# A decoder step's mixing phase: the inverse as a task of its own, the delta rule later behind q's tile, block turns in two parts

## The chip, the cores and the metric

The kernel runs on one core of a Trainium2 chip. The metric is device time in microseconds for one execution of the whole program; three runs of the kernel before gave 2160.1, 2160.87 and 2161.47 us. One more execution was recorded by the hardware profiler. PE is TensorE (matrix multiply), DVE VectorE, ACT ScalarE, POOL GpSimd, SP the engine that issues most DMAs.

## The reference

One step of a hybrid decoder layer, in f32: 512 new positions of one prompt and 8 single tokens of sampled sequences (520 columns), model width 2048. The mixing half is a gated delta rule with 8 heads of 128 beside a pooling group; the second half is a SwiGLU of width 5632.

```python
def decoder_layer(h, ...):
    xn = rmsnorm(h, norm_mix)
    proj = xn @ w_in                      # q | k | v | z | beta, decay | pool
    qkv_c, new_conv = short_conv(conv_buf, proj[..., :3 * DN_WIDTH], conv_w)   # 4 taps, silu
    ...
    a_mat = m + jnp.eye(CHUNK)            # m: strict lower part of (k beta) k^T * decay
    u = triangular_solve(a_mat, v * beta)
    w = triangular_solve(a_mat, k * beta * exp(g))
    # over the chunks, with the state S carried along:
    v_new = u_i - w_i @ S
    o = q_i * exp(g_i) @ S + qk_i @ v_new
    S = S * exp(g_last) + k_dec^T @ v_new
    ...
    dn_out = rmsnorm(o, dn_norm) * silu(z)
    h = h + concat([dn_out, pool_out]) @ w_out
    ...
```

## The kernel before

**Phases.** From 0 to about 605 us the kernel projects the 520 columns: 40 tiles of 128 output columns, each 96 matmuls (`product`; lines 168 to 170: a hi/lo split of both operands in three passes, over 16 blocks of the inner dimension and two column chunks of 264 and 256). The tiles' order is k0 to k3, z0 to z3, v0, q0, v1, q1, v2, q2, v3, q3, then the same for heads 4 to 7, then the eight pool tiles p6, p7, p4, p5, p2, p3, p0, p1. From about 607 us the output product follows (lines 1178 to 1180), and from about 618 to the end the SwiGLU part, which the change does not touch.

**Weave.** The delta rule and the other small work are generators on tracks of a `Weave` object (line 45). During every tile `weave.step()` is called 16 times, after the 15th matmul, then after each sixth to the 87th, then after the 90th, 93rd and 96th. A task that yields n is gone on with n steps later. A track is worked off in order, and a task starts no sooner than its delay after it was added. So these numbers decide where PE's small matmuls stand among the projection's. PE executes in this written order. The order on the other engines is set by the framework's scheduler when the program is built, with the evictions of a tile's results (line 259) and the weight splits (lines 135 and 137) at high priority. Every engine executes its list in order.

**One head.** A k tile is convolved (DVE lines 737 and 739: four taps; ACT line 740: silu) and, in `turn_blocks` (757), turned block by block: a transpose on DVE, a store to `tok_d` and four loads back, on POOL's queue. `keys` (790) forms the strict lower matrix in `mixb` and stores its four 32x32 diagonal blocks per chunk to `nd_d`. `eliminate` (822) handles four heads at once: it loads the blocks as `nb` and inverts them by 31 steps of two DVE instructions (lines 835 and 837); then `ud_d` is written twice, plain and transposed (838 and 841). `qv_tiles` (1112) loads the inverse as `utf` for a head (line 1117), projects v and q, and adds `delta(h)`, one step later, that is from the next tile's 15th matmul. `delta` (845) first completes the 128x128 inverse: one product (859), three triangular steps (869, each followed by DVE's 871 into `uu`), beside them the product of keys and q (878); then for four chunks it runs the state recurrence: S times keys (894), R on DVE (896), W (901), the output and the next state (906, 912, 913). `states`, `sample_norms`, `sample_product` and `sample_out` (988) handle the sampled tokens and stand in the first track behind the deltas; `sample_out` writes its columns of all eight heads in `mixa` (line 1013). After it DVE forms differences of mixa's halves (L203) and splits the rows for the output product (ACT 194 `xh`, DVE 195 `xl`).

```python
            qT = d1tile("s0", [P, SEQ], "qT")
            qkv_tile(0, h, qT)
            qk = d1tile("tq", [P, SEQ], "qk")
            turn_blocks(0, h, qT, qk)
            weave.add(delta(h, qT, qk, vs), 0, 1)
```

Of the kernel before, what the change touches and what calls it, by code (L numbers as in the profile page):

```python
# [17 lines left out]
P = 128  # L18
# [24 lines left out]
class Weave:  # L43
# [3 lines left out]
    def __init__(self):  # L47
        self.tracks, self.wait, self.now = ([], []), [0, 0], 0

# [20 lines left out]
def decoder_kernel(ctx, tc, x_prompt, x_sample, state_delta, state_conv, state_pool, norm_mix, w_in,  # L70
# [186 lines left out]
    def normed_out(out, acc, c0, c1, base):  # L257

        dve.tensor_tensor(out, acc[:, c0 - base:c1 - base], rb[:out.shape[0], c0:c1], op=ALU.mult)  # L259

    def columns():
        ext = pre.tile([P, 3 + SEQ], F32, tag="ext", name="ext", bufs=2)
        pool.memset(ext[:, 0:3], 0.0)
        return ext

# [255 lines left out]
    with ExitStack() as p1:  # L521
# [234 lines left out]

        def turn_blocks(kind, h, src, dst):

            bt, d = d1tile("bt", [P, SEQ], "bt"), tok_d[kind, h]
            if kind % 2:  # L760
                dve.transpose(bt, src)
                d = d.rearrange("p f -> (p f)").rearrange("(c p f) -> c p f", c=NCH, p=P)
                pool.dma_start(d.rearrange("c p f -> p c f"), v3(bt))
                rows = d.rearrange("c (i p) (j q) -> j p (c i) q", p=32, q=32)
            else:
                dve.transpose(bt.rearrange("p (j c q) -> p c j q", j=4, c=NCH),
                              src.rearrange("p (c j q) -> p c j q", j=4, c=NCH))
                pool.dma_start(d, bt)
                rows = d.rearrange("(i p) (j f) -> j p i f", p=32, j=4)
            for j in range(4):  # L770
                pool.dma_start(dst[32 * j:32 * j + 32, :].rearrange("p (n q) -> p n q", n=rows.shape[2]), rows[j])

        def decay(h):
# [16 lines left out]
        def keys(h):  # L790
# [23 lines left out]
            for q in range(4):  # L814
                r = slice(32 * q, 32 * q + 32)
                sp.dma_start(nd_d[h, q].rearrange("c s j -> s c j"), nn3[r, :, r])
            for q in range(4):
                r = slice(32 * q, 32 * q + 32)
                pool.memset(nn3[r, :, r], 0.0)


        def eliminate(b):
            hs = slice(4 * b, 4 * b + 4)
            nb = d1tile("nb", [64, 32, 32], "nb")
            sp.dma_start(nb.rearrange("p s j -> p (s j)"), nd_d[hs].rearrange("h q c s j -> (h q c) (s j)"))
            u = d1tile("u", [64, 32, 32], "u")
            uf = u.rearrange("p s j -> p (s j)")
            yield 10
            pool.memset(uf, 0.0)
            pool.memset(uf[:, 0:1024:33], 1.0)  # L830
            for t in range(31, 0, -1):
                w = 32 - t
                tm = d1tile("tm", [64, 256], "tm")
                tv = tm[:, 0:t * w].rearrange("p (s j) -> p s j", j=w)
                dve.tensor_tensor(tv, nb[:, 0:t, t:t + 1].broadcast_to([64, t, w]),
                                  u[:, t:t + 1, t:32].broadcast_to([64, t, w]), op=ALU.mult)
                dve.tensor_tensor(u[:, 0:t, t:32], u[:, 0:t, t:32], tv, op=ALU.subtract)
# [3 lines left out]
            sp.dma_start(ud_d[hs, :, 1].rearrange("h q c s j -> (h q) c (s j)"), ut.rearrange("p s j -> p (s j)"))  # L841
            yield 1


        def delta(h, qT, qk, vs):
            kT, nn, kd = mixb[:, h % 4, 0:SEQ], mixb[:, 4 + h % 4, 0:SEQ], kds[h]
            fk, ik = sck[:, h, 0, :], sck[:, h, 1, :]
            utf = utfs[h % 2]
            udf, tdf = utf[:, 0], utf[:, 1]
            gcb, dm = decay(h)  # L850
            act.activation(gcb, gcb, AF.Exp)
            qts = d1tile("qts", [P, SEQ], "qts")
            dve.tensor_tensor(qts, qT, gcb, op=ALU.mult)

            xp = pst()
# [5 lines left out]
            pool.tensor_copy(v3(cur), udf)  # L863
            yield 2
            for it in range(3):
                yp = v3(pst())
                j = slice(32 * it + 32, P)
                for c in range(NCH):
# [3 lines left out]
                                         op0=ALU.mult, op1=ALU.add)  # L872
                if it == 0:
                    dve.tensor_tensor(v3(kd), v3(kd), bc3(sck[:, h, 2, :]), op=ALU.mult)
                if it == 2:
                    gq_ = pst()
                    for c in range(NCH):
                        te.matmul(gq_[:, ck(c)], kT[:, ck(c)], qT[:, ck(c)], start=True, stop=True)
                    aq = d1tile("aq", [P, SEQ], "aq")
                    for c in range(NCH):  # L880
                        dve.scalar_tensor_tensor(aq[:, ck(c)], gq_[:, ck(c)], fk[:, c:c + 1], dm[:, ck(c)],
                                                 op0=ALU.mult, op1=ALU.mult)
                if it == 1:
                    scaled(vs, ik)
                yield 2

            op_ = pst()
            S = None
            for c in range(NCH):
                if S is None:  # L890
                    R = by_chunk(vs)[:, c]
                else:
# [5 lines left out]
                    R = Rt  # L898
                    yield 2
                wp = pst()  # L900
# [13 lines left out]
                S = S2  # L914
                yield 1
                if c == 1:
                    ss = d1tile("ss", [P, NCH], "ss")
                    junk = d1tile("junk", [P, P], "junk")
                    for j in range(NCH):
                        act.activation(by_column(junk), by_chunk(qk)[:, j], AF.Square, accum_out=ss[:, j:j + 1])  # L920
                    dve.tensor_scalar(ss, ss, EPS, None, op0=ALU.add)
# [191 lines left out]
        def qv_tiles(h):  # L1113
            utf = utfs[h % 2].rearrange("p a c j -> p (a c) j")
            for q in range(4):
                r = slice(32 * q, 32 * q + 32)
                sp.dma_start(utf[r, :, r], ud_d[h, q].rearrange("a c s j -> s (a c) j"))
# [9 lines left out]
        kds = {}  # L1127
# [978 lines left out]
```

## Time and profile before

| what | value |
|---|---|
| median of three runs | 2160.87 us |
| the profiled execution | 2161.12 us, of it span 2159.4 |
| PE busy, share of the span | 2127.0 us, 98% |
| DVE | 1772.2 us, 82% |
| ACT | 919.9 us, 43% |
| POOL | 531.4 us, 25% |
| mean granted PE clock of the execution | 0.998 |
| PE busy from 196 to 320 us | 120.82 of 124 us |
| PE busy from 480 to 595 us | 114.68 of 115 us |
| PE busy from 660 us to the end | 1489.49 of 1499 us |

A line of a time line has the start in us, the duration, engine, source line, operation and "output<-inputs"; in brackets stands the idle time of the engine before it and what ended it. A line of a table by windows has the window, its length, the busy time of PE, PE's weight loads, DVE, ACT and POOL with their instructions, PE's granted clock, the busy share of the DMA engines and GB/s. A line of the waits has who waited for what, in all, how often, and the longest. SPq is the DMA-issuing queue of SP.

### The profile page before, as it was taken

To read this page: it belongs to the slowest core of one execution; us is meant where nothing else is said; L and a number is where in the kernel's file an instruction comes from. 1 tells how busy PE (TensorE), PEld (TensorE's weight loads), DVE (VectorE), ACT (ScalarE), POOL (GpSimd) and SP (SyncE) were. 2 spreads that over 40 slices of the span, in tenths; PEclk is the share of its full clock that TensorE was granted. 3 is DMA by queue.
4 is the path that set the end of the run, shared out by engine and by line. 5 is a ranking of instruction groups with operands and counts; after the bars stand their busy time and mean duration, and the time that the engine had idled before them with its cause. 6 is when DMAs were issued, how large, how long until landed. Compare 5 with 4: busy or idle time off the path is not lost.

```text
span 2159.4 us, 43083 instructions
## 1 busy us (share of the span) xinstructions
PE 2127.0 (98%) x17681; PEld 2118.4 (98%) x17681; DVE 1772.2 (82%) x2715; ACT 919.9 (43%) x1340; POOL 531.4 (25%) x672
## 2 busy tenths in 40 slices
PE   8999999999999999999999999999999999999998
PEld 7999999999999999999999999999999999999998
DVE  7886677667599979988988988988877898887997
ACT  6433433343264544434434434434334444435444
POOL 2413441332012202233233233232113302003100
PEclk9999999999999999999999999999999999999999
DMA  8444454544445533554554454454456746438333
GB/s 281 126 125 118 130 141 122 132 125 126 122 118 162 156 114 115 150 167 141 144 164 144 143 168 142 142 169 133 121 147 189 233 112 205 115 104 248 91 108 119
DMA packets 449154, 313.84 MB, mean 145 GB/s; under 512 B 29116, under 2 KB 425813, under 8 KB 445613
## 3 DMA queue, kind: packets, MB, share of 16 engines
q1 hardware_dynamic: 422733, 219.94, 36.5%
q0 software_dynamic: 24912, 90.34, 13.4%
q8 instruction: 139, 2.28, 0.5%
q10 hardware_dynamic: 1312, 0.80, 0.1%
q14 instruction: 58, 0.48, 0.1%
HBM read 259.86 MB, written 51.82 MB: 144 GB/s over the span
## 4 chain that ended last, share of the span: by engine, by line
PE 82%; DVE 9%; DMA 3%; issue 2%; ACT 2%; POOL 1%; SPq 0%; DVEq 0%; ACTq 0%; POOLq 0%
PE dn L1252 21%; PE dn L1251 21%; PE dn L1253 21%; PE mm L168 5%; PE mm L169 5%; PE mm L170 5%; DVE lo L1245 1%; DMA vs<-tok_d 1%; DVE lo L137 1%; DVE y L739 1%; DMA st<-a_d 1%; DVE raw L1273 1%; PE dn L869 1%; DMA tok_d<-bt 1%; ACT hi L1244 0%
## 5 line engine op out<-in xcount | busy, mean ns | idle before, releaser
L1245 DVE TENSOR_TENSOR lo<-raw,hi 128x1024 fp32r<-128x1024 f32 (+1 forms) x422 | 527.9, 1271 | 89.0 <-ACT hi L1244 86.8
L1244 ACT CAST hi<-raw 128x1024 fp32r<-128x1024 f32 (+1 forms) x422 | 427.8, 1027 | 401.2 <-DVE raw L1273 195.5
L168 PE MATMUL mm<-xh,hi 128*128 128x256 f32 (+1 forms) x1280 | 380.3, 297 | 1.8 <-DVE mixa L259 1.8
L169 PE MATMUL mm<-xl,hi 128*128 128x256 f32 (+1 forms) x1280 | 362.1, 283 | 0.9 <-DVE xl L350 0.5
L170 PE MATMUL mm<-xh,lo 128*128 128x256 f32 (+1 forms) x1280 | 362.2, 283 | 0.4 <-DVE lo L137 0.4
L168 PEld LDWEIGHTS mm<-xh,hi 128*128 128x128 f32 x1280 | 242.1, 189 | 3.0 <-DVE mixa L259 2.2
L169 PEld LDWEIGHTS mm<-xl,hi 128*128 128x128 f32 x1280 | 242.3, 189 | 1.7 <-DVE xl L350 1.7
L170 PEld LDWEIGHTS mm<-xh,lo 128*128 128x128 f32 x1280 | 241.3, 189 | 0.6 <-DVE lo L137 0.6
L1252 PE MATMUL dn<-b21l,hi 128*128 128x260 f32 x620 | 175.8, 284 | 0.3 <-DVE b21l L1815 0.3
L1253 PE MATMUL dn<-b21h,lo 128*128 128x260 f32 x620 | 175.4, 283 | 0.0
L1251 PE MATMUL dn<-b21h,hi 128*128 128x260 f32 x620 | 175.0, 282 | 0.0
L1253 PE MATMUL dn<-b11h,lo 128*128 128x260 f32 x612 | 173.2, 283 | 1.3 <-DVE lo L1245 1.3
L1273 DVE TENSOR_TENSOR raw<-raw 128x1024 f32<-128x1024 f32 (+1 forms) x130 | 172.0, 1323 | 2.2
L1437 POOL TENSOR_TENSOR mixa<-mixa 128x520 f32<-128x520 f32 x22 | 50.2, 2280 | 501.6 <-DVE mixa L1431 501.6
L1252 PE MATMUL dn<-b11l,hi 128*128 128x260 f32 x612 | 173.3, 283 | 0.0
L1251 PE MATMUL dn<-b11h,hi 128*128 128x260 f32 x612 | 172.7, 282 | 0.0
L1251 PE MATMUL dn<-T1h,hi 128*128 128x260 f32 x556 | 158.1, 284 | 0.0
L1252 PE MATMUL dn<-T1l,hi 128*128 128x260 f32 x556 | 157.7, 284 | 0.0
L1253 PE MATMUL dn<-T1h,lo 128*128 128x260 f32 x556 | 156.7, 282 | 0.0
L1251 PE MATMUL dn<-B22h,hi 128*128 128x260 f32 x548 | 155.9, 284 | 0.0
L1252 PE MATMUL dn<-B22l,hi 128*128 128x260 f32 x548 | 155.6, 284 | 0.0
L1253 PE MATMUL dn<-B22h,lo 128*128 128x260 f32 x548 | 154.6, 282 | 0.4 <-DVE lo L1245 0.4
(664 smaller groups left out, 6552.6 us busy)
## 6 DMA issues: line engine op xcount, KB each, us to landing
raw<-in_w_gate_up_dram SPq DMA_DIRECT2D x134, 512.0 KB
raw<-in_w_in_dram SPq DMA_DIRECT2D x79, 512.0 KB
a_d<-mixa POOLq DMA_DIRECT2D x22, 1040.0 KB, 5.5
raw<-in_w_down_dram SPq DMA_DIRECT2D x48, 448.0 KB
mixb<-in_w_gate_up_dram SPq DMA_DIRECT2D x41, 512.0 KB
raw<-in_w_out_dram SPq DMA_DIRECT2D x25, 512.0 KB
st<-a_d POOLq DMA_DIRECT2D x49, 260.0 KB, 6.4
raw<-in_w_down_dram SPq DMA_DIRECT2D x24, 512.0 KB
```

The lines of the kernel that those rows point to most:

```text
L137: dve.tensor_tensor(lo[:, r], raw[:, r], hi[:, r].bitcast(F32), op=ALU.subtract)
L168: te.matmul(acc[ci], wh, hi[k][:, c0:c1], start=(k == 0), stop=False)
L169: te.matmul(acc[ci], wh, lo[k][:, c0:c1], start=False, stop=False)
L170: te.matmul(acc[ci], wl, hi[k][:, c0:c1], start=False, stop=(k == len(w) - 1))
L739: dve.scalar_tensor_tensor(y, ext[:, i:i + SEQ], cw(i, t), y, op0=ALU.mult, op1=ALU.add)
L1244: act.copy(hi, raw)
L1245: dve.tensor_tensor(lo, raw, hi.bitcast(F32), op=ALU.subtract)
L1251: te.matmul(acc, wh[:, k, :], xf[:, k, :], start=start and k == 0, stop=False)
L1252: te.matmul(acc, wh[:, k, :], xg[:, k, :], start=False, stop=False)
L1253: te.matmul(acc, wl[:, k, :], xf[:, k, :], start=False, stop=stop and k == wh.shape[1] - 1)
L1273: dve.tensor_tensor(r[name], r[a], r[b], op=op)
L1437: pool.tensor_tensor(q[:, 4:8:2, :], q[:, 1:4:2, :], q[:, 0:2, :], op=ALU.subtract)
```

## The change

- `delta` is cut in two. `solve(h)` completes the inverse in a track of its own; it is added before v's tile with a delay of 8 steps, or 24 for the first head of a block. Its steps stand 3, 4, 4 and 1 weave steps apart, and at its end the keys are scaled and the decay rows loaded. `delta(h)` begins with the product of keys and q, 6 steps behind q's tile (8 for the first head of a block), and its chunks have one more step of space.
- `turn_blocks` becomes the generator `turn` on a track of its own: transpose and store, then 6 steps, then the four loads. It starts 5 steps after v's and k's tiles, 9 after q's, 7 after the delta rule.
- `eliminate` yields 15 and not 10, and a copy of one column that z's second tile of the block writes (`mix[4 * b + 1]`) into the array holds it until then. The clearing of the diagonal blocks becomes a task too (`cleared`).
- The three zero columns ahead of the convolution are set once in two fixed buffers and not for each tile; the squares of q come a chunk later; the pool product of the last group waits 30 steps and not 12.

```diff
-        self.tracks, self.wait, self.now = ([], []), [0, 0], 0
+        self.tracks, self.wait, self.now = ([], [], [], [], []), [0] * 5, 0
...
+    exts = [pre.tile([P, 3 + SEQ], F32, tag="ext", name="ext", bufs=2) for _ in range(2)]
+    for ext in exts:
+        pool.memset(ext[:, 0:3], 0.0)
+
     def columns():
-        ext = pre.tile([P, 3 + SEQ], F32, tag="ext", name="ext", bufs=2)
-        pool.memset(ext[:, 0:3], 0.0)
-        return ext
+        exts.append(exts.pop(0))
+        return exts[1]
...
-        def turn_blocks(kind, h, src, dst):
+        def turn(kind, h, src, dst):
...
+            yield 6
+            if kind == 0:
+                dst = qks[h] = d1tile("tq", [P, SEQ], "qk")
             for j in range(4):
                 pool.dma_start(dst[32 * j:32 * j + 32, :].rearrange("p (n q) -> p n q", n=rows.shape[2]), rows[j])
+            if kind == 3:
+                weave.add(gate(h, dst), 3, 8)
+
+        def query_rows(h, qT):
+            yield from turn(0, h, qT, None)
+
+        def key_rows(h):
+            kds[h] = d1tile("kd", [P, SEQ], "kd")
+            yield from turn(1, h, mixb[:, h % 4, 0:SEQ], kds[h])
...
+            weave.add(cleared(h), 2, 5)
...
-            yield 10
+            yield 15
+            pool.tensor_copy(uf[:, 0:1], mix[4 * b + 1][:64, NB:NB + 1])
             pool.memset(uf, 0.0)
...
-        def delta(h, qT, qk, vs):
-            kT, nn, kd = mixb[:, h % 4, 0:SEQ], mixb[:, 4 + h % 4, 0:SEQ], kds[h]
-            fk, ik = sck[:, h, 0, :], sck[:, h, 1, :]
+        def solve(h):
+            kT, nn = mixb[:, h % 4, 0:SEQ], mixb[:, 4 + h % 4, 0:SEQ]
...
-            yield 2
+            yield 3
             for it in range(3):
...
-                if it == 2:
-                    gq_ = pst()
...
-                if it == 1:
-                    scaled(vs, ik)
-                yield 2
+                yield 4 if it < 2 else 1
+            kd = kds[h]
+            dve.tensor_tensor(v3(kd), v3(kd), bc3(sck[:, h, 2, :]), op=ALU.mult)
+            gcb, dm = decay(h)
+            act.activation(gcb, gcb, AF.Exp)
+            solved[h] = cur, gcb, dm
+
+        def delta(h, qT, vs):
+            kT, nn, kd = mixb[:, h % 4, 0:SEQ], mixb[:, 4 + h % 4, 0:SEQ], kds[h]
+            fk, ik = sck[:, h, 0, :], sck[:, h, 1, :]
+            cur, gcb, dm = solved[h]
+            gq_ = pst()
+            for c in range(NCH):
+                te.matmul(gq_[:, ck(c)], kT[:, ck(c)], qT[:, ck(c)], start=True, stop=True)
...
+            dve.tensor_tensor(qts, qT, gcb, op=ALU.mult)
+            scaled(vs, ik)
+            yield 4
...
-                    yield 2
+                    yield 3
...
-                yield 1
-                if c == 1:
+                yield 2
+                if c == 2:
...
-            turn_blocks(3, h, on, on)
-            weave.add(gate(h, on), 1, 12)
+            weave.add(turn(3, h, on, on), 2, 7)
...
+            weave.add(solve(h), 4, 8 if h % 4 else 24)
             vs = d1tile("vs", [P, SEQ], "vs")
             qkv_tile(2, h, vs)
-            turn_blocks(2, h, vs, vs)
+            weave.add(turn(2, h, vs, vs), 2, 5)
             qT = d1tile("s0", [P, SEQ], "qT")
             qkv_tile(0, h, qT)
-            qk = d1tile("tq", [P, SEQ], "qk")
-            turn_blocks(0, h, qT, qk)
-            weave.add(delta(h, qT, qk, vs), 0, 1)
+            weave.add(query_rows(h, qT), 2, 9)
+            weave.add(delta(h, qT, vs), 0, 6 if h % 4 else 8)
...
-                kds[h] = d1tile("kd", [P, SEQ], "kd")
-                turn_blocks(1, h, mixb[:, h % 4, 0:SEQ], kds[h])
+                weave.add(key_rows(h), 2, 5)
...
-                weave.add(pool_mix(t // 2, *splits[t // 2]), 1, 12 if t > 1 else 7)
+                weave.add(pool_mix(t // 2, *splits[t // 2]), 1, 30 if t == 7 else 12 if t > 1 else 7)
```

The lines move: what was 825 (nb's load), 835 and 837 (elimination), 859, 869, 878, 894, 901 and 906 is now 845, 856 and 858, 872, 882, 899, 916, 923 and 928; 739, 740, 754 and 766 are now 742, 743, 757 and 769; 1008 and 1013 are 1029 and 1034; 1117 is 1138. PE has as many matmuls as before. Head 0's first product of the inverse (859, now 872) stood behind the 15th matmul of v1's tile and stands behind the 57th of q0's; for the heads of a block after the first, the product of keys and q (878, now 899) stood behind the 51st matmul of the tile after q's and stands behind the 45th; the sample's sum (1008, now 1029) stood behind the 63rd of p0 and stands behind the 15th of p1.

The order on SP's queue around the first inverse, before, from the last keys' blocks to the loads of `utf` (645 and 647 are its two buffers; `raw` is a weight load):

```order
L816 DMA nd_d<-mixb 32x4x32 x3
L131 DMA raw<-in_w_in_dram 128x8x128
L816 DMA nd_d<-mixb 32x4x32
L776 DMA gcb<-gcr_d 128x512
L825 DMA nb<-nd_d 64x1024
L131 DMA raw<-in_w_in_dram 128x8x128 x6
L838 DMA ud_d<-u 16x4x1024
L841 DMA ud_d<-ut 16x4x1024
L131 DMA raw<-in_w_in_dram 128x8x128
L1117 DMA utf_645<-ud_d 32x8x32 x3
L131 DMA raw<-in_w_in_dram 128x8x128
L1117 DMA utf_645<-ud_d 32x8x32
```

The same place of the queue now:

```order
L838 DMA nd_d<-mixb 32x4x32 x4
L798 DMA gcb<-gcr_d 128x512
L131 DMA raw<-in_w_in_dram 128x8x128
L845 DMA nb<-nd_d 64x1024
L131 DMA raw<-in_w_in_dram 128x8x128 x6
L859 DMA ud_d<-u 16x4x1024
L862 DMA ud_d<-ut 16x4x1024
L131 DMA raw<-in_w_in_dram 128x8x128
L1138 DMA utf_645<-ud_d 32x8x32 x4
```

The four stores of the last keys' blocks follow each other, and so do the four loads of head 0's inverse; the weight load that stood among each of them has moved.

DVE's order at the end of q2's tile, before (`vs` is v, `ext` and `y` are q2's columns and taps):

```order
L934 TENSOR_TENSOR ro<-ro,fq 128x4
L936 TENSOR_TENSOR mixb<-dn,ro 128x512
L259 TENSOR_TENSOR ext<-mm,rb 128x256
L761 STREAM_TRANSPOSE bt<-mixb 128x512
L137 TENSOR_TENSOR lo<-raw,hi 128x1024
L737 TENSOR_SCALAR y<-ext,prm 128x512
L754 TENSOR_TENSOR vs<-vs,sck 128x512
L739 SCALAR_TENSOR_TENSOR y<-ext,prm,y 128x512 x3
```

The same place now:

```order
L259 TENSOR_TENSOR ext<-mm,rb 128x256
L740 TENSOR_SCALAR y<-ext,prm 128x512
L757 TENSOR_TENSOR vs<-vs,sck 128x512
L137 TENSOR_TENSOR lo<-raw,hi 128x1024
L742 SCALAR_TENSOR_TENSOR y<-ext,prm,y 128x512
L933 SCALAR_TENSOR_TENSOR S<-S,egl,dn 128x128
L742 SCALAR_TENSOR_TENSOR y<-ext,prm,y 128x512
L953 TENSOR_TENSOR so<-so,ro 128x4
L742 SCALAR_TENSOR_TENSOR y<-ext,prm,y 128x512
L954 TENSOR_SCALAR so<-so 128x4
L956 TENSOR_TENSOR ro<-ro,fq 128x4
L958 TENSOR_TENSOR mixb<-dn,ro 128x512
```

The output's scaling and turn (936 and 761, now 958 and 764) have moved behind q's taps; the scaling of v has moved ahead of the weight split.

DVE's order at the end of the mixing phase, before, from the sample's last columns of `mixa` on:

```order
L1013 SCALAR_TENSOR_TENSOR mixa<-sc_u,prm,mixa 128x8x8
L203 TENSOR_TENSOR mixa<-mixa 128x4x260 x2
L259 TENSOR_TENSOR pe_7283<-mm,rb 128x256
L1072 TENSOR_TENSOR pes<-pe_7283 128x512
L137 TENSOR_TENSOR lo<-raw,hi 128x1024
L1075 TENSOR_TENSOR pes<-pes,rcnt 128x1
L137 TENSOR_TENSOR lo<-raw,hi 128x1024
L1077 SCALAR_TENSOR_TENSOR pw<-pes,pe_7283 128x512
L195 TENSOR_TENSOR xl<-mixa,xh 128x520 x2
```

The same now, with the sample's small steps ahead of it:

```order
L1039 COPY sc_u<-dn 64x128
L195 TENSOR_TENSOR dl<-pw,dh 128x520
L220 RECIPROCAL sc_u<-sc_u 128x64
L221 TENSOR_TENSOR sc_u<-sc_u 128x64
L222 TENSOR_TENSOR sc_u<-sc_u 128x64
L223 TENSOR_SCALAR sc_u<-sc_u 128x64
L224 TENSOR_TENSOR sc_u<-sc_u 128x64
L1033 TENSOR_TENSOR sc_u<-sc_u 128x64
L1034 SCALAR_TENSOR_TENSOR mixa<-sc_u,prm,mixa 128x8x8
L203 TENSOR_TENSOR mixa<-mixa 128x4x260 x2
L137 TENSOR_TENSOR lo<-raw,hi 128x1024
L195 TENSOR_TENSOR xl<-mixa,xh 128x520
```

p0's second eviction, its pool taps and two weight splits stood behind the sample's columns and stand ahead of them; before the splits of mixa's rows (195) only one weight split is left, and p1's evictions fall among them.

More of the change, by code (lines that the diff above doesn't have):

```diff
@@ L769, in turn_blocks, with cleared @@
                 rows = d.rearrange("(i p) (j f) -> j p i f", p=32, j=4)
+            yield 6
+            if kind == 0:
+                dst = qks[h] = d1tile("tq", [P, SEQ], "qk")
             for j in range(4):
                 pool.dma_start(dst[32 * j:32 * j + 32, :].rearrange("p (n q) -> p n q", n=rows.shape[2]), rows[j])
+            if kind == 3:
[5 more added lines that the diff above has]
+            yield from turn(1, h, mixb[:, h % 4, 0:SEQ], kds[h])
+        def cleared(h):
+            nn3 = v3(mixb[:, 4 + h % 4, 0:SEQ])
+            for q in range(4):
+                r = slice(32 * q, 32 * q + 32)
+                pool.memset(nn3[r, :, r], 0.0)
+            yield 1
         def decay(h):
@@ L816, in keys @@
                 sp.dma_start(nd_d[h, q].rearrange("c s j -> s c j"), nn3[r, :, r])
-            for q in range(4):
-                r = slice(32 * q, 32 * q + 32)
-                pool.memset(nn3[r, :, r], 0.0)
+            weave.add(cleared(h), 2, 5)
         def eliminate(b):
@@ L842, in eliminate @@
             yield 1
-        def delta(h, qT, qk, vs):
-            kT, nn, kd = mixb[:, h % 4, 0:SEQ], mixb[:, 4 + h % 4, 0:SEQ], kds[h]
-            fk, ik = sck[:, h, 0, :], sck[:, h, 1, :]
+        def solve(h):
+            kT, nn = mixb[:, h % 4, 0:SEQ], mixb[:, 4 + h % 4, 0:SEQ]
             utf = utfs[h % 2]
             udf, tdf = utf[:, 0], utf[:, 1]
[L850 to L853, printed above, removed]
             xp = pst()
@@ L872, in delta @@
                                          op0=ALU.mult, op1=ALU.add)
-                if it == 0:
-                    dve.tensor_tensor(v3(kd), v3(kd), bc3(sck[:, h, 2, :]), op=ALU.mult)
-                if it == 2:
-                    gq_ = pst()
[L877 to L882, printed above, removed]
-                if it == 1:
-                    scaled(vs, ik)
-                yield 2
+                yield 4 if it < 2 else 1
[11 more added lines that the diff above has]
+                te.matmul(gq_[:, ck(c)], kT[:, ck(c)], qT[:, ck(c)], start=True, stop=True)
+            aq = d1tile("aq", [P, SEQ], "aq")
+            for c in range(NCH):
+                dve.scalar_tensor_tensor(aq[:, ck(c)], gq_[:, ck(c)], fk[:, c:c + 1], dm[:, ck(c)],
+                                         op0=ALU.mult, op1=ALU.mult)
+            qts = d1tile("qts", [P, SEQ], "qts")
+            dve.tensor_tensor(qts, qT, gcb, op=ALU.mult)
+            scaled(vs, ik)
+            yield 4
             op_ = pst()
@@ L919, in delta @@
                     for j in range(NCH):
-                        act.activation(by_column(junk), by_chunk(qk)[:, j], AF.Square, accum_out=ss[:, j:j + 1])
+                        act.activation(by_column(junk), by_chunk(qks[h])[:, j], AF.Square, accum_out=ss[:, j:j + 1])
                     dve.tensor_scalar(ss, ss, EPS, None, op0=ALU.add)
@@ L1117, in qv_tiles @@
                 sp.dma_start(utf[r, :, r], ud_d[h, q].rearrange("a c s j -> s (a c) j"))
+            weave.add(solve(h), 4, 8 if h % 4 else 24)
             vs = d1tile("vs", [P, SEQ], "vs")
             qkv_tile(2, h, vs)
[L1120 removed]
+            weave.add(turn(2, h, vs, vs), 2, 5)
             qT = d1tile("s0", [P, SEQ], "qT")
             qkv_tile(0, h, qT)
[L1123 to L1127 removed]
+            weave.add(query_rows(h, qT), 2, 9)
+            weave.add(delta(h, qT, vs), 0, 6 if h % 4 else 8)
+        kds, qks, solved = {}, {}, {}
         for b in range(2):
```

## The prediction

> **What bounds the kernel now.** I read the page's first part, then busy time by stage, then TensorE's waits, and last the time lines at each wait.
>
> ```profile
> PE 2127.0 (98%) x17681; PEld 2118.4 (98%) x17681; DVE 1772.2 (82%) x2715; ACT 919.9 (43%) x1340; POOL 531.4 (25%) x672
> ```
>
> ```profile
> core 0: us, PE busy (x) PEld busy (x) DVE busy (x) ACT busy (x) POOL busy (x), PEclk, DMA share, GB/s
> 132.00:196.00 64.00, 57.67 (x465) 57.12 (x464) 46.02 (x105) 18.97 (x39) 15.61 (x28) 0.95 0.43 115
> 320.00:480.00 160.00, 158.78 (x1349) 158.03 (x1348) 116.14 (x276) 61.79 (x113) 44.42 (x86) 1.00 0.47 126
> 595.00:660.00 65.00, 63.48 (x523) 62.75 (x523) 62.81 (x96) 37.99 (x58) 11.32 (x14) 1.00 0.46 132
> ```
>
> TensorE (PE) is busy 98% of the span, so an edit that removes no matmul can only win where PE stands still or runs at a lower clock, and it loses wherever PE now meets something that isn't ready. The change removes no matmul. In the part it touches, one stage stands out: 132 to 196 us, with 6.3 us of idle PE and a mean clock of 0.95. The last quoted stage matters too: from 595 to 660 VectorE (DVE) is busy for 62.81 of 65 us, so what is late on DVE there is made good by nothing.
>
> ```profile
> PE dn L859 <- DMA utf<-ud_d: 4.5, 1, 4.5
> PE dn L869 <- DVE uu L871: 3.1, 6, 0.6
> PE mm L168 <- DVE mixa L259: 1.8, 1, 1.8
> PE dn L894 <- DVE S L909: 1.6, 1, 1.6
> ```
>
> These are PE's waits from 60 to 610 us, 11 us in all. The largest is the first matmul of head 0's delta rule (L859), which waits for the inverse to come back from DRAM. It also costs clock:
>
> ```profile
> 162.00:163.00 1.00, 0.00 (x0) 0.00 (x0) 0.00 (x0) 0.00 (x0) 0.00 (x0) 0.81 0.82 161
> 163.00:164.00 1.00, 0.20 (x1) 0.23 (x2) 0.99 (x2) 0.00 (x0) 0.00 (x0) 0.50 1.10 324
> 169.00:170.00 1.00, 1.00 (x10) 1.00 (x10) 0.25 (x1) 0.99 (x2) 0.53 (x1) 0.78 0.21 33
> ```
>
> PE works again from 163.80 (below), and the granted clock is 0.50 until about 169.4: 5.6 us at half speed, 2.8 us lost. This loss occurs once before and once after, so it doesn't enter the sum. The Trainium skill, "TensorE: Matmul & The Clock Gate", Part 1, would have the clock back after one busy window of about 3.4 us, a loss of 1.7 us by an estimate from that page; the trace shows the longer time, and decides.
>
> **Term 1: head 0's inverse, +4.1 us.**
>
> ```profile
> 115.37 2.04 SPq L816 DMA_DIRECT2D nd_d<-mixb  x1
> 119.89 0.54 SPq L825 DMA_DIRECT2D nb<-nd_d  x1
> 123.59 0.20 DVE L835 TENSOR_TENSOR tm<-nb,u 64x31 f32<-64x31 f32 x1 [3.88 <-DMA nb<-nd_d]
> 145.57 0.28 PE L168 MATMUL mm<-xh,hi 128*128 128x264 f32 x1
> 155.01 0.18 DVE L837 TENSOR_TENSOR u<-u,tm 64x31 f32<-64x31 f32 x1
> 156.38 0.55 SPq L841 DMA_DIRECT2D ud_d<-ut  x1
> 157.30 0.28 PE L168 MATMUL mm<-xh,hi 128*128 128x264 f32 x1
> 159.63 1.32 SPq L1117 DMA_DIRECT2D utf<-ud_d  x3
> 161.05 0.40 SPq L131 DMA_DIRECT2D raw<-in_w_in_dram  x1
> 161.49 2.57 SPq L1117 DMA_DIRECT2D utf<-ud_d  x5
> 163.80 1.99 PE L859 MATMUL dn<-utf,mixb 128*128 128x96 f32 x8 [4.53 <-DMA utf<-ud_d]
> ```
>
> Before, the chain is: elimination on DVE from 123.59 to 155.01 (31 pairs with projection work between them), store of the transposed inverse at 156.38, four loads from 159.63, PE goes on at 163.80. From the last pair to PE that is 8.8 us. The changed order lets the four stores of head 3's keys (nd_d) follow each other on the DMA-issuing queue, where a weight load stood ahead of the last (issued 115.37); nb's load should come about 2 us sooner. The elimination itself keeps its 31 pairs and about as many projection instructions between them (five splits, six evictions, four convolution taps), so it still takes 31.4 us and ends near 153.1. Behind it the four loads now stand together, without the weight load at 161.05 (0.4 us): PE can go on at 153.1 + 8.4 = 161.5.
>
> But PE wants it sooner. The new task `solve(0)` has its first matmul (L872) behind 57 of the 96 matmuls of q0's tile, not behind 15 of v1's. q0's 96 matmuls run from 145.57 to 157.30, 0.122 us each, so PE gets there at 145.57 + 57 x 0.122 = 152.5 and stands for 9 us, twice the wait of before. The 39 matmuls left in q0 and 15 in v1, which ran ahead of the wait, now stand behind it: 54 x 0.122 = 6.6 us. Against before, PE is late by 161.5 + 6.6 - 163.8 = 4.3; I take **+4.1**, as the wait at v0's start (1.8) may lose a little. If nb isn't sooner at all it is +6.1, if it is 4 us sooner, +2. The half clock after the wait is paid either way.
>
> **Term 2: the other heads, -2.3 us.** The three triangular steps (L882) now stand 18 matmuls apart, not 12; the six waits before L869 (3.1 us) and the one for S (1.6), where a late decay row held DVE, go: -4.7. In their place the product of keys and queries (L899) moves forward, from behind 51 matmuls and the solve to behind 45 without it.
>
> ```profile
> 213.13 0.42 DVE L259 TENSOR_TENSOR ext<-mm,rb 128x256 f32<-128x256 f32 x1 [1.13 <-PE mm L170]
> 220.72 0.61 POOL L768 DMA_DIRECT2D tok_d<-bt  x1 [2.04 <-DVE bt L766]
> 223.61 2.27 POOL L771 DMA_DIRECT2D vs<-tok_d  x4 [0.79 <-ACT W L903]
> 227.31 0.29 PE L168 MATMUL mm<-xh,hi 128*128 128x264 f32 x1
> 228.32 0.42 DVE L259 TENSOR_TENSOR ext<-mm,rb 128x256 f32<-128x256 f32 x1
> 230.77 0.69 DVE L754 TENSOR_TENSOR vs<-vs,sck 128x512 f32<-128x512 f32 x1
> 233.73 0.63 ACT L740 ACTIVATE qT<-y 128x512 f32<-128x512 f32 x1 [3.09 <-DVE y L739]
> 237.11 1.14 PE L878 MATMUL dn<-qT,mixb 128*128 128x128 f32 x8
> DMA to landing us min/median/max: 2.5/3.9/4.3
> ```
>
> At v3 (start 227.31) q is ready 7.05 us into the tile and was used at 237.11, 2.8 us later. After, PE gets to the product after 45 x 0.12 and three woven matmuls, 6.1 us in. On DVE the eviction comes first, and at once when PE is done (as at 213.13, 0.4 us before a tile's start); the output's scaling and turn, 1.2 us, no longer stand ahead. That would have q ready 5.4 us in, in time. But v's scaling now stands behind the first tap, 0.4 us in, and its loads are later: v's turn on DVE stands behind the second chunk's remainder (R, after 39 of q's matmuls), some 7 us into q's tile where it was at 6.2; with the store's 2.8 us and the loads' 1.7 and 2.5 to 4.3 (last row, this v's four loads), v is back 0.2 to 2.3 us into the next tile. What is over 1.0 us holds q, one for one. I take 1.4: PE waits 0.4 us in each of six tiles (v2, v3, k4, v6, v7, p6), 2.4, net **-2.3**. The ends are -4.7 (no hold) and +2.5 (1.2 us each).
>
> **Term 3: the end of the mixing phase, +4.5 us.** The deltas end later in their track, so everything queued behind them there does too: the sample tasks run 8 weave steps later.
>
> ```profile
> 589.28 0.23 DVE L1010 TENSOR_SCALAR sc_u<-dn 128x64 f32<-128x64 f32 x1 [1.86 <-PE dn L1008]
> 592.92 0.29 DVE L1013 SCALAR_TENSOR_TENSOR mixa<-sc_u,prm,mixa 128x64 f32<-128x64 f32 x1
> 593.24 2.39 DVE L203 TENSOR_TENSOR mixa<-mixa 128x1040 f32<-128x1040 f32 x2
> 596.02 0.28 PE L168 MATMUL mm<-xh,hi 128*128 128x264 f32 x1
> 605.69 0.69 DVE L195 TENSOR_TENSOR xl<-mixa,xh 128x520 fp32r<-128x520 f32 x1
> 607.52 0.28 PE L1178 MATMUL mm<-xh,hi 128*128 128x260 f32 x1
> ```
>
> The last of them (`sample_out`) writes its columns of mixa (L1013, ended 593.2); then DVE forms differences (L203) and splits the eight heads (L195, the last ended 606.3) that the output product reads from 607.52, one head per 0.36 us, the eighth at 607.52 + 7 x 0.36 + 0.12 = 610.2. Margin 3.9 us. After, its matmul comes behind 15 matmuls of p1 (596.02 + 1.8 = 597.8) instead of 63 of p0 (589). DVE then has queued: one tap product, the small steps, the differences (2.4), one weight split (1.2), by which it is 606.4; eight splits at 0.61 with two evictions, a weight split and three pool instructions between them, 8.3 us, end at 614.7. PE wants the eighth at 610.2: late by **4.5**. DVE is busy for 97% of this stage, so it doesn't catch up. If a second chain were to fill in, 0; if the small steps also trail, 6.
>
> **At no cost.** The 24 POOL memsets that go are off the path, POOL being busy 25%; so are the squares of q, one chunk later on an ACT that is busy 43%; none of PE's four kinds of wait above is on either, and without that cover a memset would cost what its row on POOL shows, some 0.1 us. The six steps put between a turn's store and its loads free POOL's queue, on which the loads stood and waited for the store; their price is v's late scaling, counted in term 2. The copy that holds the elimination waits for z1's last column, which is there before nb lands. Weight loads keep their sequence on the DMA-issuing queue, and no PE wait above is on one. The elimination's later place may hold z2's or z3's start by up to 2 us, and the loads of head 4's inverse its solve by up to 1.5; both taken as 0.
>
> **Sum.** 4.1 - 2.3 + 4.5 = 6.3 us on the profiled execution's 2161.12 (span 2159.4 and 1.7 around it; the median of the three runs is 2160.87): **2167.4 us**.
>
> **Rivals.**
> - *The inverse is in time* (faster). PE stopped at 159.27 and its clock fell 3.4 us later. If the last load lands by 155.9, the wait at q0 is no longer than that and the clock may hold: term 1 is 155.9 + 6.6 - 163.8 - 2.8 = -4.1. With term 2 as it stands and the end of the phase covered that is 2154.7; with every wait gone -4.5 - 2.8 - 1.8 - 4.7 = -13.8, 2147. It decides at an elimination that ends by 147.5, 5.6 us sooner than worked out, and, with that, at a term 3 under 2 us. Against it: its start can't be much before 121, and 31 pairs don't shrink. For it: the time at which nb lands is an estimate. Chance 0.18.
> - *The heads gain and the end hides* (no change). Term 3 at 0.5 because DVE regains its 3.9 us margin: 4.1 - 2.3 + 0.5 = +2.3, 2163.4; or term 3 stands and the heads and the inverse come out at their lower ends, 2.0 - 4.7 + 4.5 = +1.8. Chance 0.22. The 97% of DVE speaks against it.
> - *The change doesn't move the inverse.* The order shows that it moves PE's request by 54 matmuls and the elimination by 2 us: it is the request that moves. That is the forecast, and a longer one if nb isn't sooner and both small holds come: 6.1 + 2.5 + 6 + 3.5 = +18.1, 2179. Chance 0.05.
>
> The Trainium skill, "TensorE: Matmul & The Clock Gate", Part 1, gives the clock's fall the same 3.4 us, in windows that run freely, so that by it a wait a little longer may pass without loss and one a little shorter may not; no run here shows either.
>
> **Range and chances.** Forecast 0.55 (2165.5 to 2176), the rivals as above. The range takes in part of the first rival and leaves out its far end and that of the last: 2154 to 2177. A measurement of this kernel tells about 0.2% (4.3 us) from no change. Faster by more 0.18, within 0.24, slower by more 0.58.
>
> **What would show it.** Term 1: PE's longest wait is about 9 us at L872 in q0's tile, followed by half clock; a wait under 3.4 us there and a clock of 1.00 would refute it. Term 2: waits of about 0.4 us at L899 on the activation of q, with DVE's scaling of v held by its loads just ahead, and none at L882. Term 3: PE waits on splits (xl) in the output product's first 3 us, DVE's L1034 near 603 in the old frame. What would make it all wrong: an elimination that starts well before nb's old time, or DVE idle behind 595.

## The result and the profile after

| | before | after |
|---|---|---|
| median | 2160.88 us (2160.1 to 2161.47, 4 runs) | 2184.43 us (2181.62 to 2185.61, 4 runs) |
| ratio after/before, 95% interval | | 1.0107 [1.009, 1.0125] |
| profiled execution, of it span | 2161.12, 2159.4 us | 2184.14, 2182.4 us |

The changed kernel is slower by 23.6 us. The forecast was 6.3 us slower, in a range of 2154 to 2177: the direction was right, the size was not, and the time lies outside that range.

The first row is from the page of the changed kernel; the two below are its busy time by windows.

```profile
PE 2132.2 (98%) x17681; PEld 2121.5 (97%) x17681; DVE 1771.5 (81%) x2715; ACT 918.4 (42%) x1340; POOL 534.5 (24%) x652
```

```profile
132.00:196.00 64.00, 54.37 (x450) 53.80 (x449) 42.86 (x96) 16.16 (x28) 8.74 (x15) 0.92 0.41 103
196.00:320.00 124.00, 116.79 (x956) 114.97 (x956) 81.49 (x196) 48.15 (x110) 45.93 (x72) 0.97 0.46 120
```

PE executes the same 17681 matmuls. It is busy 5 us longer in all, of which some 2.6 us are more time at half clock (by its clock, as shown below), and it stands idle for the rest of the 23 us. From 196 to 320 us it is now busy for 116.8 us where it was 120.8, and its mean clock there is 0.97. PE's waits up to 700 us, without those of the program's first microseconds:

```profile
PE dn L872 <- DMA utf<-ud_d: 9.0, 1, 9.0
PE dn L928 <- ACT W L925: 6.2, 4, 2.0
PE dn L899 <- ACT qT L743: 4.8, 6, 0.9
PE mm L168 <- DVE mixa L259: 4.5, 3, 2.6
...
PE mm L1199 <- DVE xl L195: 2.9, 4, 1.2
...
PE dn L916 <- DVE S L931: 0.9, 1, 0.9
```

The waits of the old triangular steps (3.1 us) and the longest for the state (1.6) are gone, as forecast. Those for utf (9 us) and for xl stand where the forecast had them. Three lines differ from it: 6.2 us for W (the result of a product that ACT copies for PE's next one), which it had at nothing; 4.5 us at the starts of column chunks (L168), where it had 1.8; and 4.8 us for q (L899), where it had 2.4.

The first matmul of a tile, before and after, shows where the time comes in (us, from the two traces' time lines):

| first matmul of | before | after | difference | growth since the row above |
|---|---|---|---|---|
| z2 | 108.97 | 109.86 | 0.9 | 0.9 |
| q0 | 145.57 | 149.76 | 4.2 | 3.3: z's tiles 2 and 3 |
| q1 | 181.87 | 191.35 | 9.5 | 5.3: head 0's inverse |
| p4 | 514.88 | 534.28 | 19.4 | 9.9: the heads |
| the output product | 607.52 | 628.09 | 20.6 | 1.2 |
| end of the span | 2159.4 | 2182.4 | 23.0 | 2.4: the output product's start |

The first 0.9 us is the landing of the program's first loads in this one execution; in two of the runs below z2 starts at 108.62 and 108.69. The stretches also don't hold the same work: in the traces 16 small matmuls more now stand from q0 to q1, 24 fewer from q1 to p4, and 8 more from p4 to the output product, roughly 0.1 us each. So the output product's row is moved work in the main, and the heads cost more than their 9.9 us.

**The wait for W.** Time lines of the changed kernel on POOL, ACT and PE, from the end of v3's tile into q3's (which starts at 256.07):

```profile
248.73 0.61 POOL L771 DMA_DIRECT2D tok_d<-bt  x1 [2.44 <-DVE bt L769]
250.35 0.76 POOL L766 DMA_DIRECT2D tok_d<-bt  x1 [1.01 <-DVE bt L764]
251.42 2.19 POOL L777 DMA_DIRECT2D qk<-tok_d  x4 [0.31 <-DMA tok_d<-bt]
...
258.99 0.31 ACT L942 ACTIVATE junk<-qk 128x128 f32<-128x128 f32 x1 [5.32 <-DMA qk<-tok_d]
259.74 1.03 ACT L135 CAST hi<-raw 128x1024 fp32r<-128x1024 f32 x1
261.41 0.25 ACT L925 COPY W<-dn 128x128 f32<-128x128 f32 x1
...
261.71 0.49 PE L928 MATMUL dn<-W,kd 128*128 128x128 f32 x2 [2.02 <-ACT W L925]
```

The loads of q2's turned blocks (`qk`) go out at 251.42, behind two stores on POOL's queue, and the first square of q (L942) starts at 258.99. Until then ACT stands for 5.3 us, and the copy of W that PE wants is behind the four squares and a weight cast in ACT's list. A wait of 2 us follows on PE. By windows, the clock behind that wait:

```profile
261.00:264.00 3.00, 2.29 (x15) 2.29 (x16) 2.96 (x5) 1.91 (x5) 1.15 (x1) 0.73 0.19 43
264.00:267.00 3.00, 3.00 (x15) 3.00 (x16) 1.70 (x6) 0.63 (x1) 0.37 (x1) 0.50 0.44 132
267.00:270.00 3.00, 3.00 (x19) 3.00 (x19) 0.97 (x2) 0.00 (x0) 0.62 (x1) 0.63 0.14 52
```

By 1 us windows the clock is at 0.50 from about 262.4 to 269.2, 6.8 us in which PE does the work of 3.4.

**The elimination's start.** Time lines of SP, DVE and PE of the changed kernel:

```profile
117.16 0.40 SPq L131 DMA_DIRECT2D raw<-in_w_in_dram  x1
117.75 0.53 SPq L845 DMA_DIRECT2D nb<-nd_d  x1
120.98 0.39 SPq L131 DMA_DIRECT2D raw<-in_w_in_dram  x1
...
125.57 0.20 DVE L856 TENSOR_TENSOR tm<-nb,u 64x31 f32<-64x31 f32 x1 [4.62 <-DMA nb<-nd_d]
126.97 0.42 DVE L259 TENSOR_TENSOR mixa<-mm,rb 128x264 f32<-128x264 f32 x1
...
127.44 0.39 PE L168 MATMUL mm<-xh,hi 128*128 128x256 f32 x1 [2.59 <-DVE mixa L259]
```

nb is asked for at 117.75, 2.1 us sooner than before (119.89), as forecast. But the first pair starts 7.8 us after that, not 3.7, and so 2 us later than before. The elimination's first instructions stand in DVE's list ahead of z2's eviction (126.97), so DVE's 4.6 us of standing for nb become 2.6 us of PE's at z3. PE reached L872 at 157.3 and went on at 166.28.

### The profile page after: what moved, and what is told of

It reads as the page before. It is cut to its first block, busy times and chain, and to the rows that moved or that the text cites. A ratio compares the mean times of both kernels' runs of the same rounds, so it can differ in the third digit from the quotient of the medians.

```text
span 2182.4 us, 43038 instructions
## 1 busy us (share of the span) xinstructions
PE 2132.2 (98%) x17681; PEld 2121.5 (97%) x17681; DVE 1771.5 (81%) x2715; ACT 918.4 (42%) x1340; POOL 534.5 (24%) x652
## 4 chain that ended last, share of the span: by engine, by line
PE 82%; DVE 8%; DMA 4%; issue 2%; ACT 2%; POOL 1%; SPq 0%; DVEq 0%; ACTq 0%; POOLq 0%
PE dn L1272 21%; PE dn L1271 21%; PE dn L1273 21%; PE mm L168 5%; PE mm L169 4%; PE mm L170 4%; DVE lo L1265 1%; DVE lo L137 1%; DMA qk<-tok_d 1%; DMA vs<-tok_d 1%; DVE y L742 1%; PE dn L882 1%; DMA st<-a_d 1%; DMA gcb<-gcr_d 1%; PE mm L1271 0%
## 5 line engine op out<-in xcount | busy, mean ns | idle before, releaser
L168 PE MATMUL mm<-xh,hi 128*128 128x256 f32 (+1 forms) x1280 | 381.3, 298 | 4.9 <-DVE mixa L259 4.5
L168 PEld LDWEIGHTS mm<-xh,hi 128*128 128x128 f32 x1280 | 243.2, 190 | 6.2 <-DVE mixa L259 5.2
```

The lines of the kernel that those rows point to most:

```text
L168: te.matmul(acc[ci], wh, hi[k][:, c0:c1], start=(k == 0), stop=False)
```

## The experiments

The kernel before was run again beside each group: its medians were 2160.65, 2160.45 and 2160.74 us. "After" below is 2184.43, and where a trace is compared, its profiled execution.

**The squares off q's blocks.** The squares are taken of the turned keys, so that ACT needn't wait for q's loads; the kernel leaves out q's norm, as the output's scale is now worked out from the keys.

```diff
-                        act.activation(by_column(junk), by_chunk(qks[h])[:, j], AF.Square, accum_out=ss[:, j:j + 1])
+                        act.activation(by_column(junk), by_chunk(kds[h])[:, j], AF.Square, accum_out=ss[:, j:j + 1])
```

> The changed kernel with the squares (L942) taken of the turned keys, which have long landed, in place of the turned q, so that nothing on ACT waits for q's turn. It leaves out q's own norm. Theory A (ACT, in order, holds the copy W behind squares that wait for q's loads): TensorE's waits at L928 for W, 6.2 us in the changed kernel, go, and the half clock after the 2.0 us wait at 260 us (3.4 us lost) goes with them: 2184.4 - 9.6 = 2174.8. Rival (W is late because its own product or the remainder R is late): L928 keeps about 6 us of waits, 2183 to 2186.

2172.11 us (2171.0 to 2173.01), ratio to before 1.0053 [1.0038, 1.0068]: 12.3 us less than after. Busy time from 196 to 320, and the waits from 60 to 640 us:

```profile
196.00:320.00 124.00, 120.18 (x1022) 119.37 (x1022) 87.71 (x209) 50.70 (x112) 47.97 (x79) 1.00 0.51 131
```

```profile
PE dn L872 <- DMA utf<-ud_d: 8.1, 1, 8.1
PE mm L168 <- DVE mixa L259: 4.9, 2, 2.7
PE dn L899 <- ACT qT L743: 4.8, 6, 1.7
```

Below these come only xl (2.7) and S (1.0). L928 is gone from the list, the clock of that stage is whole, and between the first matmuls of q3 and p4 the run is 10.2 us shorter than after: 6.2 of waits, 3.4 of half clock, and 0.6 that no wait accounts for. So the largest part of the 23 us is the order on ACT: an instruction that waits for a load, ahead of one that PE wants.

**The first heads' request later.** `solve` of each block's first head 33 steps after v's tile begins, its delta rule 14 behind q's.

```diff
-            weave.add(solve(h), 4, 8 if h % 4 else 24)
+            weave.add(solve(h), 4, 8 if h % 4 else 33)
...
-            weave.add(delta(h, qT, vs), 0, 6 if h % 4 else 8)
+            weave.add(delta(h, qT, vs), 0, 6 if h % 4 else 14)
```

> The changed kernel with solve of heads 0 and 4 at a delay of 33 steps, not 24, and their delta at 14, not 8: the first product of head 0's inverse stands behind 15 matmuls of v1, as before the change. Theory A (the request moved 54 matmuls forward while the inverse lands when it lands): the wait at L872 falls from 9.0 to about 2.4 us, 6.6 less; 2177.8, or 2175.0 if the clock holds through the shorter wait. Rival (the inverse itself is late because TensorE's own progress sets the evictions between its steps): the wait stays 7 to 9 us, 2183 or more.

2164.9 us (2163.33 to 2168.3), ratio 1.0023 [1.0013, 1.0032]: 19.5 us less, far more than either expectation. The waits from 60 to 660 us:

```profile
PE mm L168 <- DVE mixa L259: 4.2, 3, 2.6
PE dn L882 <- DVE uu L884: 2.7, 3, 0.9
PE mm L1199 <- DVE xl L195: 2.7, 3, 1.2
PE dn L899 <- ACT qT L743: 2.1, 2, 1.7
PE dn L872 <- POOL ccp L744: 1.9, 1, 1.9
PE dn L916 <- DVE S L931: 1.3, 3, 0.5
```

The wait at L872 falls from 9.0 to 1.9 (this row names a copy on POOL as the last to come): the inverse was asked for too soon. The rest came unasked. The deltas share one track, so all later heads moved too; ACT stands at the squares for q's loads 1.8 us at most, where it stood 5.3, the W waits (6.2) are gone, and those for q fall from 4.8 to 2.1.

**nb by another queue.** POOL issues its load, not SP.

```diff
-            sp.dma_start(nb.rearrange("p s j -> p (s j)"), nd_d[hs].rearrange("h q c s j -> (h q c) (s j)"))
+            pool.dma_start(nb.rearrange("p s j -> p (s j)"), nd_d[hs].rearrange("h q c s j -> (h q c) (s j)"))
```

> The changed kernel with the load of the 32x32 blocks (nb) issued from POOL's queue, not from SP's, where it stood 0.2 us of queue behind a 512 KB weight load. Theory A (a load on SP's queue lands behind the load issued ahead of it): nb lands some 4 us after its issue at 118, not 7.7 us, the elimination starts near 122 and not at 125.6; the wait of z3 for its eviction (2.6) goes and the one at L872 falls to about 7; in all -4, 2180.4. Rival (the DMA engines themselves are full then, so the queue does not matter): nb lands near 125 as it did, 2184.

2182.84 us (2180.87 to 2185.44), ratio 1.01 [1.0083, 1.0117]. nb was issued at 116.76 and the first pair started at 124.44, again 7.7 us on. The queue is not what holds it. The Trainium skill, "DMA: Bandwidth & Descriptors", section "Issuing engines are not separate DMA queues", says that transfers of all issuing engines run on the same 16 DMA engines and interleave; this run agrees.

**One weight load held back.** The load that stood 0.6 us ahead of nb (for v0's first half) waits until nb is there.

```diff
+CALLS, HELD = [], []
...
+        CALLS.append(n)
         if parts is None:
             with tc.high_priority(offset=AHEAD):
+                if len(CALLS) == 17:
+                    pool.tensor_copy(raw[0:1, 0:1], HELD[0][0:1, 0, 0:1])
                 load()
...
+            HELD.append(nb)
```

> One weight load (512 KB, raw for v's first tile), which the changed kernel issues 0.6 us ahead of nb, is held back until nb has landed; nothing else changes. Theory A, the load of nb took 7.7 us and not 3.7 since it shared the DMA engines with that weight load: the first elimination pair starts within 5 us of nb's issue, near 122, z tile 3's wait of 2.6 us is gone, the wait at L872 (9.0) falls by some 3 us, and the time is 2177 to 2180. Rival, nb's length has another cause (its own small pieces, or the stores of the blocks ahead of it): the pair still starts 7 to 8 us after the issue, the waits stay, and the time is 2184.

2179.58 us (2178.82 to 2185.64), ratio 1.0092 [1.0078, 1.0105]: 4.9 us less than after by the medians, though one of the four runs was as slow as after and the intervals overlap. Time lines of SP and DVE:

```profile
115.77 0.53 SPq L849 DMA_DIRECT2D nb<-nd_d  x1
120.57 6.83 SPq L132 DMA_DIRECT2D raw<-in_w_in_dram  x3
...
120.31 0.20 DVE L861 TENSOR_TENSOR tm<-nb,u 64x31 f32<-64x31 f32 x1 [0.92 <-DMA nb<-nd_d]
```

4.5 us from issue to use in place of 7.8, of which DVE waited 0.9, and z3's wait is gone. In the changed kernel the 1 us windows from 117 to 125 moved 86, 143, 163, 322, 285, 174, 274 and 125 GB/s, that is 1.57 MB: nb's 256 KB, a decay row's 256 KB issued at 116.26, and both weight loads, 512 KB each. In this run both weight loads went out from 120.57 on, when nb was already in use. So nb was late for the traffic around it. From z2's to q0's first matmul the run is 3.9 us shorter than after. One part fell out otherwise than expected: the wait for utf stayed, 8.7 us. The inverse's first store went out at 151.88, 5.3 us sooner, but PE came to L872 at 152.1, 5.2 us sooner as well, 3.9 by that stretch and 1.2 as z2 started sooner in this execution.

**Without the hold.** The elimination yields 10 as before, and nothing holds it to z's second tile.

```diff
-            yield 15
-            pool.tensor_copy(uf[:, 0:1], mix[4 * b + 1][:64, NB:NB + 1])
+            yield 10
```

> The inverse isn't held to z's second tile: 10 steps as before and no copy of the tile's column. Theory A, the hold costs nothing as nb's landing at 125.6 is later than it anyway and DVE's order is the same: 2184, the waits at z tiles 2 and 3 (1.6 and 2.6) stay, the first pair still starts near 125. Rival, the hold is what stands in the way (the waits of 4.2 us at z's tiles 2 and 3 and the later start of the elimination come from it): they go, and the time is 2178 to 2180.

2182.0 us (2181.27 to 2183.66), ratio 1.0098 [1.0084, 1.0112]; its interval overlaps that of after. The orders of PE, DVE and SP are those of the changed kernel, so the hold moves nothing. Of the rival's signs only one came: z3's wait is absent, z2's (2.2 us) is there. nb was issued at 117.07 and used at 122.82. Here z2's wait was followed by half clock from about 113.5 to 116.9. Counted from nb's issue, the weight split on DVE then ended 4.7 us on and not 3.2, and the second weight load, which followed the split at once in both traces, was issued 4.8 us on (121.84) and not 3.2 (120.98). That agrees with the run before: less traffic beside nb. So the theory that the hold costs nothing agrees with the time and the orders, but the first pair's start near 125, which it expected, did not come.

**The product of keys and q later.** Eight steps behind q's tile for all heads.

```diff
-            weave.add(delta(h, qT, vs), 0, 6 if h % 4 else 8)
+            weave.add(delta(h, qT, vs), 0, 8)
```

> The changed kernel with every delta 8 steps behind q's tile, not 6, so that the product of keys and q stands behind 57 matmuls and not 45. Theory A (q is ready about 0.8 us after TensorE asks for it): the six waits at L899 (4.8 us) go; the sample's tasks come two steps later and cost up to 1.5 us at the output product: 2179.6 to 2181.1. Rival (DVE is the bound of each head, so a later start only moves the wait to W, R or S): the waits at L899 go but those at L916, L923 and L928 grow by as much, 2183 to 2186.

2172.54 us (2171.0 to 2176.25), ratio 1.0058 [1.0043, 1.0073]: 11.9 us less, where a few were expected. The waits that changed, from 60 to 640 us:

```profile
PE dn L916 <- DVE S L931: 2.8, 2, 1.6
...
PE dn L899 <- ACT qT L743: 2.4, 3, 1.8
PE dn L916 <- DVE S L933: 1.6, 3, 0.6
```

The waits for q halve (4.8 to 2.4), as meant; but the larger gain is again that no wait for W is left. The squares still stand for q's loads, up to 4.9 us, but the delta rule's steps, and with them PE's demand for W, come two steps later, and the loads don't. Part is given back at the state (L916, 0.9 to 4.4).

**The end of head 7 closer.** Its two wider spacings are taken back, so `sample_out` comes earlier.

```diff
-                    yield 3
+                    yield 3 if h < 7 else 2
...
-                yield 2
+                yield 2 if h < 7 else 1
```

> In head 7 alone the two wider spacings of the changed delta rule are taken back (2 steps for 3 ahead of W, 1 for 2 behind the output), so that sample_out comes earlier again. Theory A, the waits at the start of the output product (L1199, 2.9 us, xl late) come from sample_out's later place: they fall to 0.6 us or less, and the time is 2182 (2.3 to 2.9 less than 2184.4). Rival, the splits are late for the last tile's own eviction: the waits stay within 0.5 us and so does the time, 2184. If head 7's closer steps wait for W instead, L928 and L916 waits in tiles 60 us before the end grow by up to 2 us and eat the gain.

2180.24 us (2178.31 to 2181.99), ratio 1.0088 [1.0075, 1.0102]: 4.2 us less by the medians, with intervals that overlap. No wait at L1199 is left; a wait of 1.6 us for W at p7 went as well, which the closer steps happened to avoid. But p7 stands ahead of p4, and from p4's first matmul to the end of the span this run is 4.2 us shorter than after. So the sampled columns are what the output product waited for, and the price is the 2.9 us of those waits and a little more.

**Together.** The later request, the closer end and no hold; then the later request, the closer end and the held weight load (with the hold kept).

> The inverse's consumer of the first heads later (solve 33 steps, the delta rule 14), the end of head 7 close as before, and no hold. Theory A, the costs add: 2164.9 of the run with the later consumers less 2.5 at the output product gives 2162.4, and less a further 1.5 where the clock does not fall after those waits (it did in that run, from 612 to 616) 2160.9, about the time of the kernel before (2160.7). Rival, the two are not additive, since a head's waits move with the steps: 2165 to 2167.

2161.87 us (2159.57 to 2165.43), ratio 1.0006 [0.9997, 1.0015]: the costs add, and nothing measurable is left between this and the kernel before. Its z2 and z3 waits were 2.3 and 2.6 us.

> The inverse's consumer of the first heads later (33 and 14 steps), head 7's end close as before, the hold kept, and the weight load held back until nb has landed. Theory, costs add where they don't touch: 2161.9 of the run with the first two less z tile 3's wait of 2.6 gives 2159.3; the elimination ends 5 us sooner while PE comes 2.6 sooner, so that the wait for utf (2.0) goes too: 2157.3. Rival, the later weight load makes v0's first half late, or waits of the steps grow as PE comes sooner: 2161 to 2163.

2157.3 us (2155.57 to 2160.47), ratio 0.9987 [0.9978, 0.9995]: 27.1 us less than after and 3.4 less than the kernel before. The time is the one expected, in part by luck: z3's wait went, but the one for utf, which was to go, is 1.4 us. It is 4.6 us under the run before, with intervals apart. The two differ in the hold too, but that was worth no clear time above, so the held weight load pays. The gain on the kernel before is under the 0.2% taken as the bound of a measurement, though the interval leaves out 1. Waits from 60 to 660 us, and busy time by windows:

```profile
PE mm L172 <- DVE mixa L263: 2.1, 1, 2.1
PE dn L904 <- ACT qT L747: 1.9, 2, 1.2
PE dn L887 <- DVE uu L889: 1.8, 2, 0.9
PE dn L877 <- DMA utf<-ud_d: 1.4, 1, 1.4
```

```profile
132.00:196.00 64.00, 62.65 (x538) 62.35 (x538) 48.39 (x105) 18.89 (x32) 13.54 (x22) 1.00 0.46 120
196.00:320.00 124.00, 121.06 (x1030) 120.28 (x1030) 91.53 (x232) 53.76 (x114) 53.36 (x88) 1.00 0.52 140
```

The stage from 132 to 196, which had 6.3 us of idle PE and a clock of 0.95 in the kernel before, has 1.4 us and a clock of 1.00.

**Two that went too far.** The same with the product of keys and q eight steps behind for every head, and that with the third triangular step one later.

> As the run before, and the product of keys and q eight steps behind q's tile for every head but the blocks' first. Theory: of the waits that the run without the held load had, those for qT (1.7) were of the blocks' ends and the waits for S (1.7) followed; a later product may take off up to 1 us, 2156 to 2157. Rival: the waits for S and W grow as in the run with this edit alone (L916 by 2 us there): 2159 to 2160.

2162.85 us (2158.73 to 2165.38), ratio 1.0007 [0.9998, 1.0016]. The rival holds in its mechanism, and the time is beyond its 2160: PE waits 4.0 us for S, a triangular step now waits 2.6 us, and half clock follows that.

> As the run before, and of the three triangular steps the third stands 5 weave steps behind the second (the first two one closer). Theory: the third step's waits for uu (2.9 us in three waits) shrink to 1 us or less: 2155. Rival: the second step then waits for uu as much, or the third step's place at a tile's end was not the cause: no difference from the run before.

2165.98 us (2161.45 to 2168.64), ratio 1.002 [1.0011, 1.0029]. The triangular steps still wait 4.1 us in three waits, S 4.6: the spacing at a tile's end wasn't their cause. What is, no run here shows.

## Why the prediction was off

- **"At no cost": the squares of q.** This is the step that failed, with 10.2 us. The text argued that ACT is busy 43% and that none of PE's four kinds of wait was on an edit of this group. But those waits were those of the old order. A low share says that ACT has time, not that what stands ahead of W's copy in its list is ready. The working counted the six steps between a turn's store and its loads as a gain for POOL's queue, and didn't follow the later loads to their reader, the squares, and from there to the copy behind them. With the loads out of it the waits are gone, and that run, at 2172.11 us, is inside the range.
- **The half clock.** The text kept it out of the sum: one loss before, one after. A second one of 3.4 us came with the wait for W, and is in the 10.2. The one at L872 cost about 2.0 us behind the wait, which ended at 166.28 with the clock back by about 170.2, where it had cost 2.8.
- **Term 1, head 0's inverse.** Mechanism right: a wait of 9.0 us at L872 where 9 was forecast, and PE's idle time from q0 to q1 grew from 4.5 to 9.3 us, 4.8 against 4.1, inside its ends. (The stretch grew by 5.3, but it holds 16 small matmuls more.) nb's issue came 2.1 us sooner as said. The landing didn't: the 3.7 us from issue to use of the old trace was carried over, though the load now goes out 0.6 us behind a weight load; weight loads stood under "at no cost". Holding that one back gives 4.5.
- **"z2's or z3's start by up to 2, taken as 0".** 3.3 us net, and put at nothing without a reason. The waits are 1.6 us at z2, 2.6 at z3 and 0.35 at v0, less the 1.8 that stood at v0 before. z3's is nb's late landing, passed on by DVE's order; z2's is not from the hold, without which it was 2.2. The trace has z1's eviction at 112.60 in DVE's list, behind decay products that stood 0.7 us for their load and a weight split of 1.2 us; no run takes these away.
- **Term 2, the other heads.** The waits that were to go went. Those for q are 0.8 us each and not 0.4. At v3 the loads of v came 1.9 us into the tile (1.4 was taken), and a weight split of 1.2 us then stood between v's scaling and the second tap:

```profile
240.83 0.69 DVE L757 TENSOR_TENSOR vs<-vs,sck 128x512 f32<-128x512 f32 x1 [0.73 <-DMA vs<-tok_d]
241.44 1.22 DVE L137 TENSOR_TENSOR lo<-raw,hi 128x1024 fp32r<-128x1024 f32 x1
242.58 0.74 DVE L742 SCALAR_TENSOR_TENSOR y<-ext,prm,y 128x512 f32<-128x512 f32 x1
...
245.06 0.63 ACT L743 ACTIVATE qT<-y 128x512 f32<-128x512 f32 x1 [1.88 <-DVE y L742]
245.75 1.16 PE L899 MATMUL dn<-qT,mixb 128*128 128x128 f32 x8 [0.56 <-ACT qT L743]
```

  Six waits of 4.8 us in all and 0.9 that is left for S, less 4.7 removed: 1.0 lost, where 2.3 was to be gained.
- **Term 3, the end of the mixing phase.** Mechanism and place right (L1199, xl late, DVE's last step for the samples at 623.19), size 2.9 us of waits for 4.5; taking it back made the stretch from p4 to the end 4.2 shorter.
- **The rivals.** None of the three had a mechanism near this. The longest put 2179 together out of upper ends and had no wait for W in it, so its nearness to 2184 is luck.

The waits and the clock named here come to some 21 of the traces' 23 us, with the first loads' 0.9; the rest is not assigned.

## What to carry to other kernels

When an instruction is moved, follow each load that it issues to its first reader, and then ask which engine's list that reader stands in and what PE wants from behind it: a free engine with one unready instruction at its head is as late as a full one. A transfer's time from an old trace holds only with the old neighbours; look at what is issued within a microsecond or two of its new place. And a wait of one or two microseconds on PE should be priced with the clock that may follow it.

## What the runs showed of the hardware

PE's clock fell after waits far shorter than the 4.5 us of before, and not after all of them. A window of the changed kernel that holds z3's wait of 2.59 us (up to 127.44), and one of the run with the closer end behind the same wait, there 2.84 us up to 126.30:

```profile
125.00:129.00 4.00, 1.56 (x13) 1.56 (x14) 3.16 (x13) 0.53 (x2) 0.00 (x0) 1.00 0.02 6
```

```profile
126.00:130.00 4.00, 3.70 (x18) 3.70 (x19) 3.62 (x13) 1.78 (x3) 0.00 (x0) 0.57 0.00 0
```

The first lost no clock (nor in the microseconds behind it); the second, at a mean of 0.57 over 4 us, had some 3.4 us at half speed. At z2 a wait of 2.16 us was followed by half clock in one run and one of 2.27 us was not in another. The shortest that was followed by it was 1.19 us, at the output product, with one of 0.48 us 1.8 us ahead of it. The same two waits stand in seven traces, and in four of them the clock fell. Behind them, the changed kernel and the run with the later request:

```profile
632.00:636.00 4.00, 3.81 (x31) 3.52 (x30) 4.00 (x8) 1.41 (x3) 0.00 (x0) 1.00 0.40 114
```

```profile
612.00:616.00 4.00, 4.00 (x22) 3.97 (x22) 4.00 (x7) 1.63 (x3) 0.00 (x0) 0.57 0.43 120
```

Away from L872 the half speed lasted about 3.4 us, or twice that, each time, and behind the waits of 8 to 9 us at L872 three times that, the wait's end included. The Trainium skill, "TensorE: Matmul & The Clock Gate", Part 1, has windows of about 3.4 us that run freely: the lengths and the chance in them agree. By its rule (no idle gaps above about 3.4 us) these waits should be safe, and some of them are not.
